# Modulation rows summed in the values stage, and a quarter of the retention gate made by block products

## The chip, the cores and the metric

The kernel runs on one core of a Trainium2 chip. The metric is the device time of one execution in microseconds (us). The engines of the core are called PE (TensorE, matrix products), DVE (VectorE), ACT (ScalarE), POOL (GpSimd) and SP (SyncE, which here does nothing but issue DMAs, one after the other). Each engine works through its own instructions in order.

## What is computed

One decoder block over a sequence of 1024 tokens, width 1024, float32. A conditioning vector gives six modulation vectors; the input is normalized and modulated to h; then two branches, retention and dilated attention, are gated, merged and followed by an MLP. What matters here, cut from the reference:

```python
mod = jax.nn.silu(c) @ w_ada[l] + b_ada[l]
sh1, sc1, g1, sh2, sc2, g2 = jnp.split(mod, 6, axis=-1)
h = modulate(rms_norm(x, norm1_g[l]), sh1, sc1)
...
proj = h @ w_in                                  # rq, rk, rv, rg, then attention and gates
rq = rotary(heads(rq, RET_HEADS), pos)
rk = rotary(heads(rk, RET_HEADS), pos) * (RET_DK ** -0.5)
ro = retention(rq, rk, heads(rv, RET_HEADS))     # 4 heads, chunks of 128 tokens, a state handed on
...
ro = (ro * gn_g.astype(jnp.float32) + gn_b.astype(jnp.float32)).astype(h.dtype)
ret_out = (jax.nn.silu(rg) * ro) @ w_ret_out
```

`mod` has 6 x 1024 values, held as 48 columns of 128: "row" i below is the block of w_ada (128 x 1024, 512 KB) that gives column i. Rows 0 to 15 (sh1, sc1) are needed for h; rows 16 to 47 (g1, sh2, sc2, g2) only after the attention. The retention gate rg has 2048 columns: 4 heads of four blocks of 128.

## The kernel before

**Products.** Every operand is split into a high and a low half (ACT rounds the high one, DVE subtracts for the low one), and a product is three matmuls (`mm3`, L203): low by high, high by low, high by high. A plain projection block of 128 columns (`proj_mm`, L472) takes 8 k x 2 token halves x 3 = 48 matmuls of 128 x 128 by 512. Pairs of blocks can be made in the other way, by seven products instead of eight of half-size blocks (`Blocks`, L226): 7 x 4 x 3 = 84 matmuls for two blocks of columns, with sums of weight blocks and of results done by DVE.

**Order of stages.** The order is written out by hand. After the first values come the *queries and keys* (`queries_keys`, L1216): 20 pairs from the list `PAIRS` (L1138), retention (r), attention (a, k) and gates (g), each by seven products. A result is finished in `a_out` (L1167); those that are not used at once are stored in DRAM. Then the *retention values* (`values`, L1339): ten items i, five products for each of two head pairs, in four slots p of 12 matmuls each. After `v_mm(i, p)` the loop runs `v_post` of the slot before (L1298) and the weight split of the next item: `v_w` on ACT (L1274) in the slots 0 and 1, `v_low` on DVE (L1280) in 1 and 2. The results of the products s3 and 22, in a high and a low half, go to a tile `vo` and from there to DRAM. For the first head pair these are items 2 and 3, and their tiles come from the pool `raw` (L1315); later ones come from other memory. At item 7 the first loads of the next stage are started.

Then the *chunks* (`chunk`, L692): 4 heads x 8 chunks of 128 tokens. In each, PE makes the chunk's key-value products (`kv`), a part of a gate block `rg` (plain, 8 k over two chunks), the scores of the next chunk (`s_kt`, L630), the output `o` from state and scores, the transpose of the last chunk's output (`on_T`, L669) and another part of the gate. DVE updates the state, splits it, and normalizes `o`; in the first four chunks of the next head, `u_final` (L680) multiplies by the gate tile `srg` (L689). With each chunk go the loads of its step (L1393): a gate weight in every other chunk and about one modulation row per chunk, which `mod_prep` (L461) multiplies by the conditioning vector and sums, one pass of DVE over 1024 elements.

**Buffers.** The pool for loaded weights and rows, tag `raw`, has three buffers of 512 KB (`wraw`, L150). A tile takes a buffer that an earlier tile has given up, in the order of the program, and what writes it waits until the earlier tile's last use is over, a store in DRAM included. The chunks' tiles lie on the memory that the values' tiles (`x`, 26 buffers) had (`open_ret`, L508; `chunk_tiles`, L620).

Of the kernel before, what the change touches and what calls it, by code (L numbers as in the profile page):

```python
# [21 lines left out]
H = 4  # L22
# [118 lines left out]
def block_kernel(ctx, tc, io, stop=None, dbg=None):  # L141
# [24 lines left out]
    def ps_mm(name):  # L166
        return PS["p"].tile([P, 2, 512], F32, tag="mm", bufs=2, name=name)
# [436 lines left out]
    def flat(ps):  # L604
        return ps.rearrange("p a b -> p (a b)")
# [14 lines left out]
    def chunk_tiles():  # L620

        p = R["p"]
        R["j"] = p.tile([P, 2, 4, C], F32R, tag="j", bufs=2, name="j2")
        R["sm"] = p.tile([P, C], F32, tag="sm", bufs=1, name="sm00")
        for n in ("smh", "sml"):
            R[n] = p.tile([P, C], F32R, tag=n, bufs=2, name=n + "00")
        for n in ("kh", "kl"):
            R[n] = p.tile([P, 2, P], F32R, tag=n, bufs=1, name=n + "00")

    def s_kt(i):  # L630

# [48 lines left out]
    def u_final(h, es=range(4), queue=nc.sync):  # L680
        for e in es:
# [7 lines left out]
            nc.vector.tensor_mul(t, t, hd["srg", h, e])  # L689
            queue.dma_start(y_d[h][:, 2 * (i % 2):2 * (i % 2) + 2, e // 2], t.rearrange("p (t x) -> p t x", t=2))  # L690

    def chunk(h, c, ahead, w=None):  # L692
        p = R["p"]
        g = NC * h + c
        if g + 3 < NG:
            fetch(g + 3)
        if c % 2 == 0:
            hd["rgw"] = w
            hd["rgp"] = ps_mm(f"rg{h}{c}")

        ks = {0: (5, 6, 6), 1: (6, 7, 8)}.get(g) or [4 * (c % 2) + i for i in (0, 2, 4)]
        if g == 0:
            proj_mm(hd["rgp"], hd["rgw"], range(2))
            s_kt(0)
            proj_mm(hd["rgp"], hd["rgw"], range(2, 5))
        vh, vl = hd["v", g][:, 0], hd["v", g][:, 1]
        st, sh, sl = R["state"], R["sh"], R["sl"]
        kvs = []
        if c < NC - 1:
            kh, kl = hd["k", g]  # L710
            for i in range(2):
                kv = ps_s(f"kv{h}{c}{i}")
                mm3([kv], (kh[:, i, :], kl[:, i, :]), [(vh, vl)], True, True)
                kvs.append(kv)
        if g == 0:
            s_kt(1)
        proj_mm(hd["rgp"], hd["rgw"], range(*ks[:2]))
# [12 lines left out]
        if 0 < g < NG - 1:  # L730
            s_kt(g + 1)
        po = ps_s(f"o{h}{c}")
        if c > 0:
            t = hd["j", g]
            for i in range(2):
                mm3([po], (t[:, 0, i, :], t[:, 1, i, :]), [(sh[:, i, :], sl[:, i, :])], i == 0, False)
        mm3([po], hd["s", g], [(vh, vl)], c == 0, True)
        for i in range(2) if g == 0 else ():
            nc.scalar.copy(st[:, i, :], kvs[i])
        if g > 0 and c < NC - 1:  # L740
            for i in range(2):
# [28 lines left out]
    va_d = [dram.tile([S, 512], F32, name=f"vad{g}") for g in range(3)]  # L770
    aq_d = {(p, g, a): dram.tile([P, S], F32, name=f"aqd{p}{g}{a}") for p in range(2) for g in range(3) for a in range(2)}
    ak_d = {(p, a): dram.tile([P, S], F32, name=f"akd{p}{a}") for p in range(2) for a in range(2)}
    h12_d = [dram.tile([P, 2, 512], F32, name=f"h12d{m}") for m in range(4)]
    xn, wa = [], []

# [359 lines left out]
    a_pairs = [("a", g, p) for p in range(2) for g in range(3)]  # L1135
    g_pairs = [("g", i) for i in range(len(GATES) // 2)]
    k_pairs = [("k", 2, p) for p in range(2)]
    PAIRS = [{"r": r_pairs, "a": a_pairs, "g": g_pairs, "k": k_pairs}[i].pop(0) for i in "rargrarkrargrarkgaga"]  # L1138
    NA = len(PAIRS)
    OA = {}  # L1140

    def a_load(q, part):
        pair = PAIRS[q]
        src = io[{"g": "w_gate2", "a": "w_aq", "k": "w_ak2"}.get(pair[0]) or f"w_r{pair[1]}"]
# [22 lines left out]
    def a_out(q, n, x, y=None):  # L1167

        pair = PAIRS[q]
        if q not in OA:  # L1170
            OA[q] = [x4(f"qa{q}{i}") for i in range(2)]
        i, t = int(n[0]) - 1, int(n[1]) - 1
        o, view = OA[q][i][:, 512 * t:512 * t + 512], lambda z: z
        if pair[0] in "ak" and pair[1] == 1:
            o = OA[q][i].rearrange("p (r n i) -> p r n i", r=4, n=2)[:, :, t, :]
            view = lambda z: z.rearrange("p (i r) -> p r i", r=4)
        elif pair[0] in "ak" and pair[1] == 2:
            o = OA[q][i].rearrange("p (r i) -> p r i", r=8)[:, :, 64 * t:64 * t + 64]
            view = lambda z: z.rearrange("p (i r) -> p r i", r=8)
        f = AF.Sigmoid if pair[0] == "g" else AF.Copy  # L1180
        if y is None:
            nc.scalar.activation(o, view(x), f)
        else:
            (nc.vector.tensor_add if n == "12" else nc.vector.tensor_sub)(o, view(x), view(y))
            if pair[0] == "g":
                nc.scalar.activation(o, o, f)
        if n in ("12", "21"):
            if pair[0] == "g":
                dst = gate_d[GATES[2 * pair[1] + i]]
            elif pair[0] == "a":  # L1190
                dst = aq_d[pair[2], pair[1], i]
            elif pair[0] == "k":
                dst = ak_d[pair[2], i]
            else:
                return
            nc.sync.dma_start(dst, OA[q][i])
# [136 lines left out]
    def v_base_load(hp):  # L1333

        for j in range(2):
            V["m", hp, j] = t = x4(f"vm{hp}{j}")
            nc.sync.dma_start(t.rearrange("p (a b) -> p a b", a=2), m11_d[hp][:, 2 * j:2 * j + 2])

    def values(ahead):  # L1339
        last = len(VSEQ) - 1  # L1340
        for i, (hp, n) in enumerate(VSEQ):
            if i + 2 <= last:
                v_load(i + 2)
            for p in range(4):
# [32 lines left out]
        for g in (1, 2):  # L1377
# [7 lines left out]
    steps.add(more_values, manual=True)  # L1385
    steps.add(queries_keys, manual=True)

    later_mods = [G1 + k for k in range(NK)] + [SH2 + k for k in range(NK)] + \
                 [SC2 + k for k in range(NK)] + [G2 + k for k in range(NK)]
# [1432 lines left out]
def pack(x, c, w_ada, b_ada, norm1_g, w_in, rel_bias, ret_gn_g, ret_gn_b,  # L2822
# [17 lines left out]
        "w_rg": _cols(w[:, 4096:6144]),  # L2840
# [33 lines left out]
```

## Time and profile before

| | before |
|---|---|
| time, median of 3 runs | 2176.75 us (2176.67 to 2182.43) |
| time of the profiled execution | 2179.79 us |
| its span in the profile | 2178.0 us |
| PE busy | 2151.7 us, 99% |
| DVE busy | 1512.8 us, 69% |
| ACT busy | 947.4 us, 43% |
| DMA, all queues | 420.98 MB, mean 193 GB/s |

The profile shows one execution: the instructions of each engine with their start, their length, and what ended the wait before them. A row such as `L464 DVE ... raw<-raw,cb` names the line of the kernel, the engine, and the tile written and those read. "To landing" is the time from the issue of a DMA until its data are there. PE's busy time counts overlapping matmuls once, so it says when PE had work, not how fast the work went; the granted clock (PEclk, 1.0 is full) says that.

### The profile page before, as it was taken

To read this page: it belongs to the slowest core of one execution; us is meant where nothing else is said; L and a number is where in the kernel's file an instruction comes from. 1 tells how busy PE (TensorE), PEld (TensorE's weight loads), DVE (VectorE), ACT (ScalarE), POOL (GpSimd) and SP (SyncE) were. 2 spreads that over 40 slices of the span, in tenths; PEclk is the share of its full clock that TensorE was granted. 3 is DMA by queue.
4 is the path that set the end of the run, shared out by engine and by line. 5 is a ranking of instruction groups with operands and counts; after the bars stand their busy time and mean duration, and the time that the engine had idled before them with its cause. 6 is when DMAs were issued, how large, how long until landed. Compare 5 with 4: busy or idle time off the path is not lost. (4 is left out here: it accounts for less than half of the span.)

```text
span 2178.0 us, 27354 instructions
## 1 busy us (share of the span) xinstructions
PE 2151.7 (99%) x10060; PEld 1789.6 (82%) x10060; DVE 1512.8 (69%) x2361; ACT 947.4 (43%) x1741; POOL 167.2 (8%) x199
## 2 busy tenths in 40 slices
PE   8999999999999999999999999999999999999998
PEld 6888888888887888888888888888778888888887
DVE  5885777776346787785657644777876665877855
ACT  5553322323343354455657625434454445533413
POOL 0001111100002121211110000001000000000003
PEclk9999999999999999999999999999999999999999
DMA  9759998833568455546777275653244435645322
GB/s 383 282 212 311 270 334 255 235 110 116 184 240 295 160 203 182 173 168 196 205 192 209 98 260 196 222 188 136 66 179 153 153 136 195 248 138 174 109 87 78
DMA packets 161522, 420.98 MB, mean 193 GB/s; under 512 B 27877, under 2 KB 55788, under 8 KB 158316
## 3 DMA queue, kind: packets, MB, share of 16 engines
q1 hardware_dynamic: 149112, 370.70, 47.7%
q0 software_dynamic: 9584, 48.24, 9.8%
q8 instruction: 79, 1.29, 0.2%
q10 hardware_dynamic: 2692, 0.30, 0.1%
q14 instruction: 55, 0.45, 0.1%
HBM read 322.03 MB, written 158.23 MB: 221 GB/s over the span
## 5 line engine op out<-in xcount | busy, mean ns | idle before, releaser
L207 PE MATMUL qap<-hh,qaw 128*128 128x512 f32 x240 | 93.4, 389 | 0.0
L209 PE MATMUL qap<-hl,qaw 128*128 128x512 f32 x240 | 93.4, 389 | 0.0
L211 PE MATMUL qap<-hh,qaw 128*128 128x512 f32 x240 | 93.4, 389 | 0.0
L617 POOL TENSOR_TENSOR j<-qk,j 128x512 fp32r<-128x512 f32 x32 | 43.2, 1351 | 457.5 <-ACT j L616 457.5
L2193 POOL TENSOR_TENSOR accnf<-accnf,sqnf 128x256 f32<-128x256 f32 (+1 forms) x18 | 16.6, 921 | 609.6 <-ACT sqnf L2189 609.6
L2297 ACT ACTIVATE a<-a 128x512 f32<-128x512 f32 x48 | 30.3, 631 | 73.3 <-DVE a L2296 73.3
L2505 ACT CAST w2h<-w2s 128x512 fp32r<-128x512 f32 x36 | 22.4, 621 | 78.7 <-DVE w2s L2543 71.8
L264 DVE TENSOR_TENSOR fw<-w1r,fw 128x512 fp32r<-128x512 f32 x48 | 32.9, 688 | 33.5 <-ACT fw L254 33.5
L209 PEld LDWEIGHTS qap<-hl,qaw 128*128 128x128 f32 x240 | 45.0, 188 | 9.4
L211 PEld LDWEIGHTS qap<-hh,qaw 128*128 128x128 f32 x240 | 45.0, 188 | 9.3
L207 PEld LDWEIGHTS qap<-hh,qaw 128*128 128x128 f32 x240 | 45.0, 188 | 9.3
L652 ACT COPY sm<-sT 128x128 f32<-128x128 f32 x32 | 8.5, 265 | 98.9 <-PE sT L640 91.4
L2028 DVE TENSOR_TENSOR rwl<-rwl,rwh 128x1024 fp32r<-128x1024 f32 x25 | 30.2, 1221 | 29.0 <-ACT rwh L2058 29.0
L207 PE MATMUL fp<-h2h,fw 128*128 128x512 f32 x128 | 50.0, 391 | 0.0
L211 PE MATMUL fp<-h2h,fw 128*128 128x512 f32 x128 | 49.8, 389 | 0.0
L209 PE MATMUL fp<-h2l,fw 128*128 128x512 f32 x128 | 49.8, 389 | 0.0
L207 PE MATMUL roa<-rh,rwl 128*128 128x512 f32 x128 | 49.8, 389 | 0.0
L209 PE MATMUL roa<-rl,rwh 128*128 128x512 f32 x128 | 49.8, 389 | 0.0
L211 PE MATMUL roa<-rh,rwh 128*128 128x512 f32 x128 | 49.8, 389 | 0.0
L1561 ACT ACTIVATE P<-P,ng 128x128 f32<-128x128 f32 (+1 forms) x96 | 41.9, 438 | 17.5 <-DVE ng L1553 17.5
L264 DVE TENSOR_TENSOR qaw<-wa,qaw 128x512 fp32r<-128x512 f32 x60 | 40.0, 686 | 8.8 <-ACT qaw L254 8.8
L292 DVE TENSOR_TENSOR qat<-qat,qap 128x512 f32<-128x512 f32 x20 | 13.7, 687 | 46.4 <-PE qap L211 46.4
(3094 smaller groups left out, 7241.4 us busy)
## 6 DMA issues: line engine op xcount, KB each, us to landing
v<-vd SPq DMA_DIRECT2D x32, 512.0 KB, 4.3
raw<-in_w_ada_dram SPq DMA_DIRECT2D x32, 512.0 KB, 5.0
w1r<-in_w_ff_dram SPq DMA_DIRECT2D x32, 512.0 KB, 4.6
yt<-y POOLq DMA_DIRECT2D x24, 512.0 KB, 7.4
xsd<-as SPq DMA_DIRECT2D x24, 512.0 KB, 2.9
w2r<-in_w_ff2s_dram SPq DMA_DIRECT2D x24, 512.0 KB, 6.7
em<-in_w_ada_dram SPq DMA_DIRECT2D x16, 512.0 KB, 10.2
wrvs<-in_w_rv_dram POOLq DMA_DIRECT2D x16, 512.0 KB, 9.6
```

Of the source, the lines that this page charges most:

```text
L207: nc.tensor.matmul(o, wl, xh, start=first, stop=False, skip_group_check=skip)
L209: nc.tensor.matmul(o, wh, xl, start=False, stop=False, skip_group_check=skip)
L211: nc.tensor.matmul(o, wh, xh, start=False, stop=last, skip_group_check=skip)
L264: nc.vector.tensor_sub(t[:, 512:], src, fv(t[:, :512]))
L292: nc.vector.tensor_sub(u, u, b)
L617: nc.gpsimd.tensor_sub(t[:, 1], src, fv(t[:, 0]))
L652: nc.scalar.copy(sm, ps[:, :C])
L1561: nc.scalar.activation(v, v, AF.Exp, bias=ng[:, blk:blk + 1], accum_out=st[:, g, blk, 2 + a:3 + a])
L2028: nc.vector.tensor_sub(lo, fv(lo), fv(hi))
L2193: (nc.vector if f == 7 else nc.gpsimd).tensor_add(G["acc", key], G["acc", key], sq)
L2297: nc.scalar.activation(o, o, AF.Relu)
L2505: nc.scalar.copy(hi, src)
```

## The change

Three things change together.

1. *The gate.* Of the four gate blocks of a head, the last is taken out of the chunks. The four blocks so taken (one per head) form two pairs, kind "s", at the end of `PAIRS`; they are made by seven products with the queries and keys, go through Silu and are stored in `srg_d`. In chunk 6 of each head the finished block is loaded (512 KB). The chunks do 24 k per head instead of 32, three per chunk (other numbers in head 0), and a gate weight is loaded at chunks 0, 2 and 5.
2. *The modulation rows.* 29 of the 32 rows 16 to 47 are loaded and summed in the values stage: six in each of the items 0 and 1, five in each of the items 4, 5 and 6, two in item 7. `values_mod(i)` starts the load of row i and does the pass of the row before the last one. The additions of the bias become one for all. Three rows stay in the chunks.
3. *The order of the chunks' first tiles.* `j` (two buffers of 4 KB per partition) is taken after the small tiles `sm`, `smh`, `sml`, `kh`, `kl` instead of before.

```diff
     def chunk_tiles():
...
-        R["j"] = p.tile([P, 2, 4, C], F32R, tag="j", bufs=2, name="j2")
         R["sm"] = p.tile([P, C], F32, tag="sm", bufs=1, name="sm00")
...
+        R["j"] = p.tile([P, 2, 4, C], F32R, tag="j", bufs=2, name="j2")
...
+    RG = ((6, 2, 2, 3, 3, 3, 3, 2),) + ((3,) * NC,) * (H - 1)
+
+    def rg_mm(n):
+        for _ in range(n):
+            if hd.get("rgk", NK) == NK:
+                hd["rgk"], hd["rgw"], hd["rgp"] = 0, hd["rgws"].pop(0), ps_mm("rg")
+            proj_mm(hd["rgp"], hd["rgw"], [hd["rgk"]])
+            hd["rgk"] += 1
+            if hd["rgk"] == NK:
+                hd["rgs"] = hd["rgp"]
+
+    def rg_out(h, c):
+        if "rgs" in hd:
+            e = {1: 0, 2: 0, 4: 1, 5: 1, 7: 2}[c]
+            hd["srg", h, e] = etile(f"srg{h}{e}")
+            nc.scalar.activation(hd["srg", h, e], flat(hd.pop("rgs")), AF.Silu)
+        if c == 6:
+            hd["srg", h, 3] = etile(f"srg{h}3")
+            nc.sync.dma_start(hd["srg", h, 3], srg_d[h])
...
-        proj_mm(hd["rgp"], hd["rgw"], range(*ks[:2]))
+        rg_mm(1 if g == 0 else RG[h][c] - 1)
...
-        proj_mm(hd["rgp"], hd["rgw"], range(*ks[1:]))
+        rg_mm(0 if g == 0 else 1)
...
-        if c % 2 == 1:
-            hd["srg", h, c // 2] = etile(f"srg{h}{c // 2}")
-            nc.scalar.activation(hd["srg", h, c // 2], flat(hd["rgp"]), AF.Silu)
+        rg_out(h, c)
...
-    PAIRS = [{"r": r_pairs, "a": a_pairs, "g": g_pairs, "k": k_pairs}[i].pop(0) for i in "rargrarkrargrarkgaga"]
+    s_pairs = [("s", i) for i in range(H // 2)]
+    PAIRS = [{"r": r_pairs, "a": a_pairs, "g": g_pairs, "k": k_pairs, "s": s_pairs}[i].pop(0)
+             for i in "rargrarkrargrarkgagass"]
...
+    MODS = [(i, p) for i in (0, 1, 4, 5, 6, 7) for p in range(4) if i < 7 or p < 2
+            for _ in range(2 if i < 2 and p % 2 or p == 3 else 1)]
+    NV = len(MODS)
+
+    def values_mod(i):
+        if i < NV:
+            t = V["mod", i] = wraw.tile([P, 1024], F32, tag="raw", name=f"vmod{i}")
+            nc.sync.dma_start(t, io["w_ada"][G1 + i])
+        if i > 1:
+            t, m = V.pop(("mod", i - 2)), G1 + i - 2
+            nc.vector.scalar_tensor_tensor(t, t, 1.0, cb, op0=ALU.mult, op1=ALU.mult, accum_out=mods[:, m:m + 1])
+        if i == NV + 1:
+            m = mods[:, G1:G1 + NV]
+            nc.vector.tensor_add(m, m, vec[:, VC_BADA + G1:VC_BADA + G1 + NV])
...
     def values(ahead):
...
                 if p == 2 and i < last:
                     v_low(i + 1, 1)
+                for j, at_ in enumerate(MODS):
+                    if at_ == (i, p):
+                        values_mod(j)
+                if (i, p) == MODS[-1]:
+                    values_mod(NV)
+                    values_mod(NV + 1)
...
-                      ([wsplit(io["w_rg"][4 * h + c // 2])] if c % 2 == 0 else []) +
-                      [mod_load(later_mods[8 * h + i]) for i in ({0: (0, 1), 1: ()}.get(8 * h + c, (c,)))],
+                      ([wsplit(io["w_rg"][3 * h + (0, 2, 5).index(c)])] if c in (0, 2, 5) else []) +
+                      ([later_mod()] if h > 0 and c == 4 else []),
```

More of the change, by code (lines that the diff above doesn't have):

```diff
@@ L696, in chunk @@
             fetch(g + 3)
[L697 to L701, printed above, removed]
+        if w is not None:
+            hd.setdefault("rgws", []).append(w)
         if g == 0:
-            proj_mm(hd["rgp"], hd["rgw"], range(2))
+            rg_mm(2)
             s_kt(0)
-            proj_mm(hd["rgp"], hd["rgw"], range(2, 5))
+            rg_mm(3)
         vh, vl = hd["v", g][:, 0], hd["v", g][:, 1]
@@ L772, in block_kernel @@
     ak_d = {(p, a): dram.tile([P, S], F32, name=f"akd{p}{a}") for p in range(2) for a in range(2)}
+    srg_d = [dram.tile([P, S], F32, name=f"srgd{h}") for h in range(H)]
     h12_d = [dram.tile([P, 2, 512], F32, name=f"h12d{m}") for m in range(4)]
@@ L1143, in a_load @@
         pair = PAIRS[q]
-        src = io[{"g": "w_gate2", "a": "w_aq", "k": "w_ak2"}.get(pair[0]) or f"w_r{pair[1]}"]
+        src = io[{"g": "w_gate2", "a": "w_aq", "k": "w_ak2", "s": "w_rg2"}.get(pair[0]) or f"w_r{pair[1]}"]
         i = 2 * pair[1] + pair[2] if pair[0] == "a" else pair[-1]
@@ L1179, in a_out @@
             view = lambda z: z.rearrange("p (i r) -> p r i", r=8)
-        f = AF.Sigmoid if pair[0] == "g" else AF.Copy
+        f = {"g": AF.Sigmoid, "s": AF.Silu}.get(pair[0], AF.Copy)
         if y is None:
@@ L1184, in a_out @@
             (nc.vector.tensor_add if n == "12" else nc.vector.tensor_sub)(o, view(x), view(y))
-            if pair[0] == "g":
+            if pair[0] in "gs":
                 nc.scalar.activation(o, o, f)
@@ L1193, in a_out @@
                 dst = ak_d[pair[2], i]
+            elif pair[0] == "s":
+                dst = srg_d[2 * pair[1] + i]
             else:
@@ L1386, in block_kernel, with later_mod @@
     steps.add(queries_keys, manual=True)
-    later_mods = [G1 + k for k in range(NK)] + [SH2 + k for k in range(NK)] + \
-                 [SC2 + k for k in range(NK)] + [G2 + k for k in range(NK)]
+    late_mods = iter(range(G1 + NV, 48))
+    def later_mod():
+        return mod_load(next(late_mods))
     for h in range(H):
@@ L2839, in pack @@
         "w_rv": _vblocks(w[:, 2048:4096]),
-        "w_rg": _cols(w[:, 4096:6144]),
+        "w_rg": _cols(w[:, 4096:6144].reshape(1024, 4, 4, P)[:, :, :3].reshape(1024, 1536)),
+        "w_rg2": _pairs(w[:, 4096:6144].reshape(1024, 4, 4, P)[:, :, 3].reshape(1024, 512)),
         "w_aq": _pairs(att[:, :, 0].reshape(1024, 1536)),
```

## The prediction

> **What bounds the kernel now.** First the page, for how full each engine is:
>
> ```profile
> span 2178.0 us, 27354 instructions
> PE 2151.7 (99%) x10060; PEld 1789.6 (82%) x10060; DVE 1512.8 (69%) x2361; ACT 947.4 (43%) x1741; POOL 167.2 (8%) x199
> ```
>
> TensorE (PE) is busy for all but 26 us, so a gain must be a matmul less or a part of those 26 us, and a loss is any wait that PE doesn't have today. Next the busy time by stretch around the stages that change: queries and keys until 561, retention values until 671, chunks until 985.
>
> ```profile
> core 0: us, PE busy (x) PEld busy (x) DVE busy (x) ACT busy (x) POOL busy (x), PEclk, DMA share, GB/s
> 190.00:555.00 365.00, 365.00 (x1612) 302.20 (x1612) 262.29 (x408) 104.17 (x183) 34.92 (x49) 1.00 0.73 226
> 583.00:605.00 22.00, 22.00 (x99) 18.22 (x98) 11.86 (x15) 8.70 (x12) 0.00 (x0) 1.00 0.63 220
> 671.00:701.00 30.00, 26.32 (x117) 20.96 (x118) 15.47 (x36) 11.36 (x25) 3.75 (x4) 0.94 0.73 258
> 701.00:985.00 284.00, 284.00 (x1386) 236.29 (x1385) 227.88 (x477) 132.26 (x336) 53.53 (x57) 1.00 0.53 176
> ```
>
> PE is full in each but the first chunks (671 to 701), where 3.7 us are missing and the granted clock is 0.94. VectorE (DVE) is at 54% in the middle of the values stage, so 29 more passes seem to have room there; it is at 80% in the chunks, from where they come. Last the timeline of PE, for what one matmul costs. A duration is 0.39, but they overlap; the starts count.
>
> ```profile
> 402.90 0.39 PE L207 MATMUL qap<-hh,qaw 128*128 128x512 f32 x1
> 403.13 0.39 PE L209 MATMUL qap<-hl,qaw 128*128 128x512 f32 x1
> ...
> 805.33 0.61 PE L207 MATMUL rg<-hh,raw_6146l 128*128 128x512 f32 x2
> ...
> 808.05 0.28 PE L638 MATMUL sT<-j 128*128 128x256 f32 x1
> ```
>
> In the queries and keys it is 0.227 us from start to start, and in the chunks twelve gate matmuls take 808.05 - 805.33 = 2.72, the same 0.227. A slot of the values stage (item i, part p: twelve matmuls) is 2.72 us, an item of four slots 10.9.
>
> **The matmuls: -5.4 us.** A gate block is 8 x 6 = 48 matmuls; four blocks fewer in the chunks are 192. Two pairs by seven products add 2 x 7 x 12 = 168. So 24 go, 24 x 0.227 = 5.4 us. The pairs' sums, splits and results lie under PE work where VectorE has 262 of 365 us busy: I cost them at nothing (uncovered, 14 splits by the row below, 0.69 each, would be 10 us). The pairs' two stores and the four loads of finished gate rows in chunk 6 are spread over stages whose DMA share is 0.5 to 0.7: nothing.
>
> ```profile
> L264 DVE TENSOR_TENSOR qaw<-wa,qaw 128x512 fp32r<-128x512 f32 x60 | 40.0, 686 | 8.8 <-ACT qaw L254 8.8
> ```
>
> **The chunks: 0.** They lose 192 x 0.227 = 43.6 us of PE work, so VectorE must be tested as the bound.
>
> ```profile
> L464 DVE SCALAR_TENSOR_TENSOR raw<-raw,cb x32: 1216/1218/1221, 659.5 to 972.1; 128x1024 f32<-128x1024 f32 x32
> L464 DVE DVE_READ_ACCUMULATOR raw<-raw,cb x32: 80/82/85, 660.6 to 973.2; 128x1 f32 x32
> ```
>
> ```profile
> 800.32 0.16 DVE L466 TENSOR_TENSOR mods<-mods,vec 128x1 f32<-128x1 f32 x1
> ```
>
> A row costs VectorE 1.22 + 0.08 + 0.16 = 1.46 there. With about 28 rows and four weight splits (1.22) less, VectorE falls from 228 to 228 - 41 - 5 = 182 us and PE from 284 to 240, so its share goes from 80% to 76%: still behind PE. I take 0; the bad end is 6 us, half a microsecond in each of the twelve chunks that also have a final multiply (L689).
>
> **The start of the chunks: -2 us.** Who is waited for at 671 to 701:
>
> ```profile
> PE kv L207 <- DVE kl L666: 3.1, 2, 2.5
> ```
>
> ```profile
> ACT sm L652 <- DMA vd<-vr: 7.4, 1, 7.4
> ```
>
> ```profile
> 681.00:686.00 5.00, 4.63 (x17) 3.92 (x18) 0.97 (x4) 0.68 (x3) 0.00 (x0) 0.66 1.03 352
> ```
>
> `sm` takes the memory of a tile whose store (`vd<-vr`) has not landed; behind it ACT's split of `kT` is late, `kl` too, PE idles 2.5 us, and in the five microseconds after that the granted clock is 0.66, another 0.34 x 5 = 1.7 us. The change puts the small tiles on other bytes and starts two 512 KB loads fewer ahead of them (three weights and one, for two weights and four rows). That could take away all 4.2 us, none, or, if the new place is held longer, cost up to 3. I take half the gain, 2.
>
> **The values stage: where I expect the time to go.** All loads here go through the pool `raw`, which has three buffers (L150). Today only the results of items 2 and 3 of the first head pair use it (L1315): eight tiles, one per slot, three in turn. The change runs the modulation rows through the same three buffers, with each pass two rows behind its load, and has no rows in items 2 and 3. At the end of item 1 rows 10 and 11 are loaded and not yet summed; their passes come in item 4. So **two of three buffers are held through items 2 and 3, and eight results share one.** Each must have landed in DRAM before ACT may write the next. What such a result costs today:
>
> ```profile
> 586.02 0.69 DVE L1322 TENSOR_TENSOR vr<-vr,va 128x512 f32<-128x512 f32 x1 [8.07 <-PE va L211]
> ...
> 586.74 0.62 ACT L1323 CAST vo<-vr 128x512 fp32r<-128x512 f32 x1 [1.89 <-DVE vr L1322]
> ...
> 588.12 6.54 SPq L1326 DMA_DIRECT2D vd<-vo  x3
> ...
> 606.96 0.60 ACT L1317 ACTIVATE vo<-va 128x512 fp32r<-128x512 f32 x1 [3.19 <-DMA vd<-vo]
> ...
> 610.17 1.22 DVE L1283 TENSOR_TENSOR vwl<-vwl,vwh 128x1024 fp32r<-128x1024 f32 x1
> ...
> 615.74 0.39 PE L207 MATMUL vc<-vwh,xat 128*128 128x512 f32 x1
> ```
>
> ```profile
> DMA to landing us min/median/max: 2.6/7.2/12.0
> ```
>
> ```profile
> aqd<-qa SPq DMA_DIRECT2D x12, 512.0 KB, 3.1
> ...
> y<-on SPq DMA_DIRECT2D x12, 512.0 KB, 3.2
> ```
>
> From ACT's copy to the issue of the store is 588.12 - 586.74 = 1.4 us; the stores of this line land after 2.6 to 12 us. A turn of a single buffer is thus 1.4 + landing, 4.0 at the least, against 2.72 for a slot. Even with three buffers the last two of the eight wait for a store today (606.96: 3.19 us). Stores of the same size in quieter stages land after 3.1 and 3.2; with only one result under way at a time I take 3.2 for six of the seven turns, and the median 7.2 for the one that meets the weight and base loads around item 3's start: 7 x 1.4 + 6 x 3.2 + 7.2 = 36.2 us from the first result's copy to the eighth's.
>
> The first result is late too. Ten passes stand ahead of it on VectorE, and item 0 starts when other loads are being issued:
>
> ```profile
> 564.42 0.93 SPq L1272 DMA_DIRECT2D vwl<-wrvs  x2
> ```
>
> ```profile
> raw<-in_w_ada_dram SPq DMA_DIRECT2D x32, 512.0 KB, 5.0
> ...
> vwl<-wrvs SPq DMA_DIRECT2D x12, 512.0 KB, 6.5
> ```
>
> The first row is issued at about 565.4 and lands after some 6.5, at 572. A buffer is then loaded (5.0) and read (1.3) before its next load, three in turn: one pass per 2.1 us. The tenth ends at 572 + 9 x 2.1 + 1.3 = 592.2, and the result's first operation, which was at 586.0, is 6.2 late (bounds 0, if loads keep pace, and 13).
>
> So the eighth copy is at 592.9 + 36.2 = 629.1 instead of 606.96. Behind it on ACT is the weight split of item 5, behind it on VectorE the split's low half (610.17 to 611.4 today: 4.4 after that copy) and now row 10's pass (1.3): PE can start item 5 at 629.1 + 5.7 = 634.8, not at 615.74. That is **+19.1 us**. With every store at 2.6 and no lateness: 586.74 + 28 + 5.7 = 620.4, +4.7. With 7.2 each: 592.9 + 60.2 + 5.7 = 658.8, +43.1. From item 4 on there are five rows an item, 5 x 1.3 us of VectorE beside results and weight splits, and SP's in-order queue has row loads ahead of weight loads; at the end two passes wait for loads just issued. I add 3 (0 to 9).
>
> **Sum:** -5.4 + 0 - 2 + 19.1 + 3 = +14.7 us. On the profiled execution (2179.8, of which 2178.0 are span) that is 2194.5; it lies 3.0 above the median of the runs, so on the median I say 2176.75 + 14.7 = **2191.4**.
>
> **Rivals.** (1) *The single buffer doesn't bind*, because the pool hands out memory otherwise than I read it, and the rows go where VectorE has room: -5.4 - 4.2 = 2167.2. For it: VectorE's 54%. Against it: three buffers, two of them unread, by the order of the code. This one ends faster. (2) *It binds but is mostly covered*: stores at 2.6, no lateness, -5.4 - 2 + 4.7 = 2174.1. For it: the first `vo` store today lands after 2.6; against it, the loads in the way. (3) *Stores as slow as today's median*: -5.4 - 2 + 43.1 + 3 = 2215.5. Against it: that median was measured with several in flight. (4) *The clock falls in the gaps*: as at 681, where 2.5 us idle cost 1.7 more. If three gaps of that length stand ahead of items 3, 4 and 5, 3 x 1.7 = 5 more: 2196.4. The Trainium skill (TensorE: Matmul & The Clock Gate, Part 1) has the array at half clock after one idle window of about 3.4 us, and for about as long after work resumes. This trace shows less idle time as enough (2.5 us). By the rule as written only gaps over 3.4 us would count. (5) *VectorE bounds the chunks*: up to 6 more, 2197.4; 182 of 240 us speaks against it.
>
> **Chances.** My forecast 0.54, (4) 0.08, (5) 0.02, (3) 0.13, (2) 0.10, (1) 0.13. About 0.3%, 6.5 us, is what a measurement tells from no change: below 2170.2 is faster, 0.13; (2) lies within, 0.10; the rest, 0.77, is slower. The forecast's own range is 2183 to 2206. For 8 in 10 I leave out (1) and the upper half of (3): 2173 to 2214.
>
> **What would show it.** Right: ACT's wait for `vd<-vo` (6.1 us in two waits today) grows to some 15 to 25 us in seven; PE has idle time in the values stage, ahead of items 4 and 5, and DVE waits for `raw` loads in items 0 and 1; the stage is 120 to 135 us long instead of 110; PE has 24 matmuls fewer; the chunks as a whole take about 44 us less, without a new wait. Wrong: the results of items 2 and 3 follow each other at 2.7 us, or PE waits for `onm`, `sml` or `statel` in the chunks. If the queries-and-keys stage grows by more than 38 us (168 x 0.227), my free cover there was none.

## The result, and the profile after

The changed kernel takes 2214.49 us (median of 4 runs, 2213.65 to 2215.37), beside 2176.71 for the kernel before on the same chip: 1.017 times as long, with a 95% interval of 1.0158 to 1.0183. That is 37.8 us slower; the prediction said 14.7 slower, with a range that ended at 2214.

The page of the changed kernel, its first lines:

```profile
span 2213.3 us, 27355 instructions
PE 2154.4 (97%) x10036; PEld 1787.2 (81%) x10036; DVE 1524.5 (69%) x2361; ACT 953.2 (43%) x1757; POOL 167.9 (8%) x199
```

PE has its 24 matmuls fewer (10036 for 10060) and is idle for 59 us of the span instead of 26. The busy time by stretch shows where: the queries and keys, the first 22 us of the values stage, its end, and its last 10 us together with the chunks.

```profile
core 0: us, PE busy (x) PEld busy (x) DVE busy (x) ACT busy (x) POOL busy (x), PEclk, DMA share, GB/s
190.00:593.50 403.50, 403.50 (x1782) 334.21 (x1781) 284.55 (x440) 117.69 (x205) 34.92 (x49) 1.00 0.70 215
599.50:621.50 22.00, 18.45 (x82) 14.97 (x81) 9.82 (x13) 9.82 (x15) 0.00 (x0) 1.00 0.84 282
709.50:739.50 30.00, 20.41 (x83) 16.18 (x82) 20.87 (x30) 9.59 (x14) 6.33 (x7) 0.89 0.78 270
739.50:1022.50 283.00, 277.36 (x1357) 228.91 (x1356) 207.89 (x433) 136.23 (x355) 59.08 (x66) 1.00 0.50 167
```

The queries and keys are still full. The values stage, full before, now has holes at its start (second row) and at its end (third row, two thirds). The chunks, from 749.6 on, lack a little too. The length of each stage, from the start of its first matmul to the start of the next stage's:

| stage, us | before | after | difference |
|---|---|---|---|
| up to the queries and keys | 180.5 | 180.7 | +0.1 |
| queries and keys | 380.8 | 418.9 | +38.1 |
| values, with the step to the chunks | 109.7 | 150.0 | +40.3 |
| chunks | 315.8 | 273.2 | -42.6 |
| the rest, to the last matmul | 1184.4 | 1184.0 | -0.4 |

The sum is +35.5, beside 35.3 between the two spans (2213.3 - 2178.0), which also hold what comes behind the last matmul. The two profiled executions, 2179.79 and 2215.37 us, are 35.6 apart; the first is 3.1 above its median and the second 0.9 above its own, which makes the 37.8 of the medians.

The waits of the values stage that the prediction named, VectorE and ACT of the changed kernel (total, number, longest):

```profile
DVE vmod L1372 <- DMA vmod<-in_w_ada_dram: 19.9, 13, 4.2
...
ACT vo L1339 <- DMA vd<-vo: 15.6, 4, 5.5
...
ACT vo L1345 <- DMA vd<-vo: 13.5, 3, 6.2
```

ACT waits seven times for a result's store, 29.1 us. In the kernel before it was two times:

```profile
ACT vo L1317 <- DMA vd<-vo: 6.1, 2, 3.2
```

ACT's timeline in the changed kernel shows the chain, first copy and eighth:

```profile
633.55 0.62 ACT L1345 CAST vo<-vr 128x512 fp32r<-128x512 f32 x1 [6.64 <-DVE vr L1344]
...
641.35 0.62 ACT L1345 CAST vo<-vr 128x512 fp32r<-128x512 f32 x1 [6.21 <-DMA vd<-vo]
...
669.77 0.60 ACT L1339 ACTIVATE vo<-va 128x512 fp32r<-128x512 f32 x1 [3.81 <-DMA vd<-vo]
```

The first copy is 633.55 - 599.57 = 34.0 us into the stage, before 586.74 - 561.34 = 25.4: 8.6 late. From there to the eighth are 669.77 - 633.55 = 36.2 us. The timeline of PE, the longer waits and the start of item 5:

```profile
615.75 0.50 PE L209 MATMUL va<-vwlTrue,xat 128*128 128x512 f32 x1 [3.55 <-DVE vwlTrue L1307]
...
643.88 0.51 PE L209 MATMUL va<-vwl,hh 128*128 128x512 f32 x1 [3.46 <-DVE vwl L1307]
...
663.83 0.80 PE L209 MATMUL vc<-vwl,hh 128*128 128x512 f32 x1 [5.41 <-DVE vwl L1305]
...
675.43 0.39 PE L207 MATMUL vc<-vwh,xat 128*128 128x512 f32 x1
...
679.66 0.51 PE L209 MATMUL vc<-vwl,xat 128*128 128x512 f32 x1 [2.48 <-DVE vwl L1305]
...
726.95 0.79 PE L209 MATMUL va<-vwl,hh 128*128 128x512 f32 x1 [8.29 <-DVE vwl L1307]
```

Every one of them is a wait for the low half of a weight, which VectorE makes late. An item has two such halves: the first is needed at its second matmul, the other at its eighth. For the first wait shown, VectorE stood 4.24 us for a row's load, made the pass at 613.32 and the low half only at 614.47. Item 5 starts 75.86 us into the stage instead of 54.40: +21.5. Behind that another 18.8 are lost, 8.29 of them in the last wait. What VectorE does ahead of it:

```profile
719.85 1.23 DVE L1372 SCALAR_TENSOR_TENSOR vmod<-vmod,cb 128x1024 f32<-128x1024 f32 x1 [1.75 <-DMA vmod<-in_w_ada_dram]
...
722.33 1.23 DVE L1372 SCALAR_TENSOR_TENSOR vmod<-vmod,cb 128x1024 f32<-128x1024 f32 x1 [1.25 <-DMA vmod<-in_w_ada_dram]
...
725.68 1.22 DVE L1307 SCALAR_TENSOR_TENSOR vwl<-vwl,vwh 128x1024 fp32r<-128x1024 f32 x1
```

These are the last two rows, summed in the same slot in which the last load was started, and only then, behind a result, the second low half for item 8. The clock falls behind the longer gaps, by the busy time by stretch:

```profile
644.60:648.00 3.40, 3.40 (x10) 2.62 (x9) 1.29 (x2) 0.62 (x1) 0.00 (x0) 0.50 0.21 78
...
661.70:668.50 6.80, 4.67 (x11) 3.71 (x12) 2.51 (x3) 0.81 (x2) 0.00 (x0) 0.50 0.34 135
...
723.10:729.90 6.80, 2.95 (x7) 2.37 (x8) 4.97 (x9) 1.58 (x3) 0.00 (x0) 0.50 0.53 155
```

PE works 3.40 + 4.67 + 2.95 = 11.0 us at half the clock, which costs half of that, 5.5; 4.0 of it lies ahead of item 5. PE's waits for low halves in the stage are 31.4 us in all (16.2 up to item 5), so waits and clock together are 36.9 of the 40.3.

### The profile page after: what moved, and what is told of

It is laid out like the page before. It is cut to its first block, busy times and chain, and to the rows that moved or that the text cites. A ratio compares the mean times of both kernels' runs of the same rounds, so it can differ in the third digit from the quotient of the medians.

```text
span 2213.3 us, 27355 instructions
## 1 busy us (share of the span) xinstructions
PE 2154.4 (97%) x10036; PEld 1787.2 (81%) x10036; DVE 1524.5 (69%) x2361; ACT 953.2 (43%) x1757; POOL 167.9 (8%) x199
## 5 line engine op out<-in xcount | busy, mean ns | idle before, releaser
L209 PE MATMUL qap<-hl,qaw 128*128 128x512 f32 x264 | 102.8, 389 | 0.0
L211 PE MATMUL qap<-hh,qaw 128*128 128x512 f32 x264 | 102.8, 389 | 0.0
L207 PE MATMUL qap<-hh,qaw 128*128 128x512 f32 x264 | 102.8, 389 | 0.0
L209 PEld LDWEIGHTS qap<-hl,qaw 128*128 128x128 f32 x264 | 49.6, 188 | 10.3
L207 PEld LDWEIGHTS qap<-hh,qaw 128*128 128x128 f32 x264 | 49.6, 188 | 10.3
L211 PEld LDWEIGHTS qap<-hh,qaw 128*128 128x128 f32 x264 | 49.6, 188 | 10.2
L1372 DVE SCALAR_TENSOR_TENSOR vmod<-vmod,cb 128x1024 f32<-128x1024 f32 x29 | 35.3, 1223 | 20.3 <-DMA vmod<-in_w_ada_dram 19.9
## 6 DMA issues: line engine op xcount, KB each, us to landing
wrvs<-in_w_rv_dram POOLq DMA_DIRECT2D x16, 512.0 KB, 10.3
```

Of the source, the lines that this page charges most:

```text
L207: nc.tensor.matmul(o, wl, xh, start=first, stop=False, skip_group_check=skip)
L209: nc.tensor.matmul(o, wh, xl, start=False, stop=False, skip_group_check=skip)
L211: nc.tensor.matmul(o, wh, xh, start=False, stop=last, skip_group_check=skip)
L1372: nc.vector.scalar_tensor_tensor(t, t, 1.0, cb, op0=ALU.mult, op1=ALU.mult, accum_out=mods[:, m:m + 1])
```

## The experiments

The theory after the result (A): the rows cost the time where they went, by waits and not by work: two of three `raw` buffers are held through items 2 and 3, passes stand in VectorE's queue waiting for their loads ahead of the weights' low halves, and the clock falls in the gaps. The rivals: the gate's products cost (B), the traffic of the moved loads costs (C), VectorE's extra work costs (D). The runs below were each timed beside the kernel before on the same chip (2176.0 to 2177.5 us in all of them).

### The parts by themselves

**gate_only.** The rows stay in the chunks' steps, the gate and the order of tiles are as after.

```diff
-                for j, at_ in enumerate(MODS):
-                    if at_ == (i, p):
-                        values_mod(j)
...
-                      ([later_mod()] if h > 0 and c == 4 else []),
+                      [later_mod() for _ in range({0: 2, 1: 0}.get(8 * h + c, 1))],
```

> The gate and the order of the first tiles as in the change; the modulation rows stay in the chunks, one per chunk, as before. Theory A (the rows in the values stage cost the time: one shared buffer, passes that wait for their loads ahead of other VectorE work, and the half clock behind each gap): the values stage is back at 110 us from 150; the 24 matmuls less show. VectorE has 9.3 us of work in the twelve chunks with a row and a final multiply, where PE has 8.7, so some of the gain goes there: 2172 to 2182 us. Theory B (the gate by seven products is the cost): 2200 us or more.

Measured 2191.0 us, ratio 1.0065 (1.005 to 1.008): slower, which A did not expect. The values stage is back at 109.7 us, so the 40 us are the rows'. But the chunks take 288.9 us. PE's waits in them, and VectorE in one of them:

```profile
PE o L207 <- DVE state L744: 9.0, 14, 0.8
PE kv L207 <- DVE kl L666: 5.6, 8, 1.1
```

```profile
865.42 1.22 DVE L689 TENSOR_TENSOR on<-on,srg 128x1024 f32<-128x1024 f32 x1
866.56 1.28 DVE L744 SCALAR_TENSOR_TENSOR state<-state,kv 128x512 f32<-128x512 f32 x2
867.75 1.22 DVE L198 TENSOR_TENSOR raw_6926l<-raw,raw_6926h 128x1024 fp32r<-128x1024 f32 x1
868.89 1.22 DVE L464 SCALAR_TENSOR_TENSOR raw<-raw,cb 128x1024 f32<-128x1024 f32 x1
```

With a quarter of the gate's products gone, the final multiply of the last head (L689) stands in VectorE's queue ahead of the state that PE needs next, and the row's pass ahead of the scores and `kl`. So the move of the rows was worth 288.9 - 273.2 = 15.7 us in the chunks, and it cost 40.3 in the values stage.

**loads_only** leaves out the 29 passes (the columns get a constant), **passes_only** leaves out the 29 loads (the passes read data that is there).

```diff
-            t, m = V.pop(("mod", i - 2)), G1 + i - 2
-            nc.vector.scalar_tensor_tensor(t, t, 1.0, cb, op0=ALU.mult, op1=ALU.mult, accum_out=mods[:, m:m + 1])
+            V.pop(("mod", i - 2))
...
```

```diff
-            t = V["mod", i] = wraw.tile([P, 1024], F32, tag="raw", name=f"vmod{i}")
-            nc.sync.dma_start(t, io["w_ada"][G1 + i])
+            V["mod", i] = cs
...
```

> The change without the 29 passes: the rows are loaded into the same buffers at the same places and not read (their sums are left out, a constant stands for them). A buffer is then free when its load has landed. Theory A: no pass waits and no buffer is held through items 2 and 3, so the values stage is 110 to 116 us and the time 2169 to 2178. Theory C (traffic): the stage stays above 130 us, 2195 or more. Theory D (VectorE's work): as A.

> The change without the 29 loads: the passes stand at the same places but read a tile that is already in SBUF (the sums are then of other data). Theory A: no pass waits, no buffer is held; the values stage is 110 to 115 us, since VectorE is at most 70% busy in any item but item 4 (14 of 11 us); 2168 to 2176. Theory C (traffic): as A. Theory D (VectorE's work): the stage stays above 130 us, 2195 or more.

Measured 2182.26 (1.0024, 1.0013 to 1.0034) and 2179.78 us (1.0015, 1.0005 to 1.0024). The values stage takes 114.6 and 113.4 us. So the traffic alone (C) costs 4.9 us, the work alone (D) 3.7; together they are far from 40. What neither run has is a pass that *waits for* a load, or a buffer that such a pass holds: the rest lies there. Both times lie some 4 us above A's range. The gate part, with the rows out of the chunks, doesn't gain what I had it gain: queries and keys and chunks together give +38.1 - 42.6 = -4.5, and that only against a profile of before that had a stall in its chunks, as the next run shows.

**before_again**, the kernel before unchanged, a second profile.

> The kernel before, unchanged, for a second profile of it. Is the wait of 2.5 us at the start of its chunks, with the lower clock behind it, there in every execution? If the store that is late there is late by chance, this profile has less of it and a span of about 2175; if not, about 2178 again.

2179.5 us (one execution), span 2177.7. The chunks take 313.0 us instead of 315.8, and PE's waits in them for `kl` and the state are

```profile
PE kv L207 <- DVE kl L666: 1.4, 2, 0.7
...
PE o L207 <- DVE state L725: 0.2, 1, 0.2
```

The wait of 2.5 us with the lower clock behind it isn't there: not every execution has it. (The span is as long as in the first profile all the same; other stages took 2.5 us more.) Against this profile the chunks gain 313.0 - 273.2 = 39.8, and the gate part, with the rows out of the chunks, is worth 1.7 us.

### What the values stage waits for

**flush_two.** One edit: the two rows that lie unread through items 2 and 3 are summed at the end of item 1, so the eight results have three buffers.

```diff
-        if i > 1:
-            t, m = V.pop(("mod", i - 2)), G1 + i - 2
-            nc.vector.scalar_tensor_tensor(...)
+        done = (i - 2, 10, 11) if i == 11 else (i - 2,)
+        for j in done:
+            if ("mod", j) in V:
+                t, m = V.pop(("mod", j)), G1 + j
+                nc.vector.scalar_tensor_tensor(...)
```

> The change, but rows 10 and 11 are summed at the end of item 1 instead of in item 4, so that items 2 and 3 have all three buffers. Theory A: the seven waits of ACT for vd<-vo (29.1 us) shrink to about the 6 us of before; the eight results take about 20 us from first copy to last instead of 36.2; the first result is 5 us later, since its VectorE waits for two loads more; item 5 starts some 11 us earlier: about 2203 us. Theory C (the DMA traffic of the moved rows fills the stage): the waits move elsewhere and the time stays at 2212 to 2216. Theory D (VectorE has too much work in the stage): the same, 2212 to 2216.

Measured 2204.78 us, 1.0129 (1.0112 to 1.0146), as A said: 9.7 less. Item 5 starts 64.1 us into the stage instead of 75.9. The stage takes 135.0 us in the profiled execution, which was 3.5 us below the median, and ACT's waits for the results' stores are

```profile
ACT vo L1339 <- DMA vd<-vo: 7.8, 2, 4.6
```

**results_own.** The same buffers relieved from the other side: the results get two buffers of their own (the memory of the cosines and sines), the rows keep `raw` and all their slots.

```diff
-            t = wraw.tile([P, 2, DV], F32R, tag="raw", name=f"vo{i}{p}")
+            t = cs[:, p % 2].bitcast(F32R).rearrange("p (a b) -> p a b", a=2)
```

> The changed kernel with one edit: the eight results of items 2 and 3 go to two buffers of their own (the memory of the cosines and sines); the rows keep the three buffers of the pool raw and all their slots. A1, the one buffer left to the results costs most: ACT's waits for vd<-vo fall from 29 to under 10 us, the values stage from 150 to 133-137 us (as in flush_two), 2198-2206. A2, passes that wait for rows ahead of low halves cost most and the results' buffer lay beside that: the stage stays at 145-150 us, 2209-2214.

Measured 2203.65 us, 1.0124 (1.011 to 1.0138): A1's time. Item 5 starts 67.6 us into the stage. The stage takes 140.6 us, 4 more than A1 gave, in an execution 2.3 us above the median; ACT's waits for stores are 8.9 + 4.2 us in five, where A1 gave under 10:

```profile
ACT cossin L1339 <- DMA vd<-cossin: 8.9, 4, 4.3
ACT cossin L1345 <- DMA vd<-cossin: 4.2, 1, 4.2
```

The two runs agree in time: the one buffer is worth about 10 us, not the 19 that I gave to the stage up to item 5. Without it item 5 still starts 9.7 and 13.2 us later than before the change, since PE then waits for low halves that stand behind passes (3.41 us at 615.83 in flush_two, 4.10 at 615.99 in results_own).

**own_buffers.** The rows get the two buffers instead, in the same slots, with the pass of row i - 2 ahead of the load of row i; the results have `raw` to themselves.

```diff
-            t = V["mod", i] = wraw.tile([P, 1024], F32, tag="raw", name=f"vmod{i}")
-            nc.sync.dma_start(t, io["w_ada"][G1 + i])
+            nc.sync.dma_start(cs[:, i % 2], io["w_ada"][G1 + i])
...
```

> All 29 rows in the same slots of the values stage as in the changed kernel, but loaded into two buffers of their own (the memory of the cosines and sines, which nobody reads in this stage); the pool raw is left to the results, as before the change. A, the shared buffers: the eight results of items 2 and 3 no longer wait for one another, the waits of ACT for vd<-vo fall from 29 us to under 10 us and the values stage from 150 to 125-133 us, which gives 2188-2198. What is left above 110 us is then the passes that wait for their loads in VectorE's queue. C, the traffic of the rows, or D, VectorE's extra work: rows, bytes and passes are the same, so the time stays within 4 us of the changed kernel's 2214.

Measured 2213.45 us, 1.017 (1.0156 to 1.0184): no gain, a miss for A as I had put it. Up to item 5 it did what A says: item 5 starts 66.9 us into the stage, and PE has no wait in items 3 and 4. Before that and behind it the waits grew; from item 5 on the stage took 81.3 us instead of 74.2. The run changed two things, since the rows now have two buffers in turn and not three. SP's queue shows what that does in the first items:

```profile
604.59 17.51 SPq L1371 DMA_DIRECT2D cossin<-in_w_ada_dram  x6
622.16 0.90 SPq L1294 DMA_DIRECT2D vwl<-wrv  x2
```

Each load waits in SP's in-order queue for the pass that frees its buffer, and the weights' loads behind six of them are issued at 622. So what the results gained, the rows lost by pacing VectorE and SP.

**last_two_later.** One edit: the last two passes are issued in slot 3 of item 7 instead of slot 1, behind both low halves of item 8.

```diff
-                if (i, p) == MODS[-1]:
+                if (i, p) == (7, 3):
                     values_mod(NV)
                     values_mod(NV + 1)
```

> The changed kernel with the last two passes and the addition of the bias issued in slot 3 of item 7 instead of slot 1, that is behind both low halves of item 8's weights; nothing else differs. A, passes waiting ahead of low halves: the wait of 8.3 us ahead of item 8's first product with those halves goes, and most of the half clock of 6.8 us behind it (3.4 us worth), so the values stage takes 137-142 us instead of 150 and the time is 2202-2207. Rival, the wait there is for item 8's weights or the traffic and the pass only stands beside it: no change beyond 3 us, 2211-2215.

Measured 2208.88 us, 1.0148 (1.0131 to 1.0165); the stage takes 142.3 us, at the edge of what A gave, and the time is 5.6 less, 2 short of its range. The long wait has become

```profile
720.05 0.50 PE L209 MATMUL va<-vwl,hh 128*128 128x512 f32 x1 [2.60 <-DVE vwl L1307]
```

**flush_no_item7** goes on from flush_two: 27 rows, none in item 7, the last two summed at the end of item 6, and two rows more in chunks.

```diff
-    MODS = [(i, p) for i in (0, 1, 4, 5, 6, 7) for p in range(4) if i < 7 or p < 2
+    MODS = [(i, p) for i in (0, 1, 4, 5, 6) for p in range(4)
...
```

> The change with rows 10 and 11 summed at the end of item 1, and no rows in item 7: 27 rows in the values stage, the last two summed at the end of item 6; five in the chunks. Theory A: the wait of 7.4 us for the last two passes and the half clock behind it (6.8 us at half, 3.4) leave item 7; in item 6 results go to ACT alone and hide most of the same wait: 2193 to 2198 us, from 2204.8. Theory C or D: two rows less are 2 to 3 us, about 2202.

Measured 2201.08 us, 1.0112 (1.0097 to 1.0128), 3.7 less than flush_two where A expected 7 or more: the stage takes 133.1 us, PE waits eleven times for low halves, 16.1 us in all. The two passes still wait for loads just issued, one item earlier (1.21 and 0.91 us).

### Fewer rows, and the order of the tiles

**rows_in_cs.** 18 rows in the values stage, a load in every second slot, each pass three slots behind its load, in two buffers of their own; 14 rows in chunks without a final multiply. **rows_in_cs_jfirst** is the same with `j` taken first, as before the change. **rows_in_cs_late** is the first with the final multiply issued in the next chunk, behind the update of the state.

```diff
...
+                slot = 4 * i + p
+                if slot % 2 and 0 <= (slot - 3) // 2 < NV:
+                    row_pass((slot - 3) // 2)
+                if slot % 2 == 0 and slot // 2 < NV:
+                    row_load(slot // 2)
...
+                      ([later_mod()] if (h > 0 and c > 3 or h == 0 and c in (4, 6)) else []),
```

> The change, but only 18 rows are summed in the values stage, one in every second slot, in the 8 KB of cos and sin that are no longer needed (two buffers of their own, a row read three slots after its load is issued); the other 14 in chunks without a final multiply. Theory A: the traffic and the passes alone cost some 4 us each at 29 rows, the rest was the shared buffers and passes that stand waiting; so the values stage is 110 to 113 us, the chunks about 273 and the time 2170 to 2178. Theory C or D (traffic or VectorE's work): 18 of 29 rows still bring 0.6 of 40 us, about 2200.

> As the one with rows in the memory of cos and sin, with the order of the chunks' first tiles as before the change (j first). By my prediction the new order is worth 0 to 4.2 us at the start of the chunks; I expect 0 to 4 us more here, as a wait of PE for kl and a lower clock behind it. If the place of the tiles doesn't matter: no difference.

> As the one with rows in the memory of cos and sin, and the final multiply of a head's gate is issued after the state update of the next chunk instead of before it. If the waits of PE for the state (4.1 us in 11) come from the multiply that stands ahead of the update, they go: 4 us less than that kernel. If VectorE is simply full there, the wait moves to kl, onm or statel and the time stays.

Measured 2187.69 (1.0054, 1.0041 to 1.0066), 2187.84 (1.0055, 1.0043 to 1.0068) and 2214.12 us (1.017, 1.0156 to 1.0184), the first some 10 us above what A gave. Between the first two, the order of the tiles makes no difference. In the first, the values stage and the step to the chunks are 119.9 us, and the largest wait is at the end:

```profile
PE rg L207 <- DVE vr L1344: 6.2, 1, 6.2
```

```profile
707.61 1.23 DVE L1370 SCALAR_TENSOR_TENSOR cossin<-cossin,cb 128x1024 f32<-128x1024 f32 x1 [3.87 <-DMA cossin<-in_w_ada_dram]
```

This pass, in the last slot of item 8, waits 3.87 us for a row whose load was issued at 696.5, 11 us before, among the chunks' first loads (DMA share 1.03 to 1.07 from 700 to 708), and the last results stand behind it. The late multiply is a plain miss, 26 us slower. There, VectorE in a chunk and PE in all of them:

```profile
835.73 1.23 DVE L689 TENSOR_TENSOR on<-on,srg 128x1024 f32<-128x1024 f32 x1 [0.92 <-ACT on L687]
...
841.25 0.81 DVE L779 TENSOR_SCALAR onm<-o,ba,gr 128x512 f32<-128x512 f32 x1
```

```profile
PE kT L645 <- DVE onm L779: 20.3, 11, 2.5
```

It left its place ahead of the state and took one ahead of the normalization, for which PE waits longer.

**rows_14.** 14 rows, two per item in the slots 2 and 3, behind both low halves; each pass a whole item behind its load, none after item 7; the other 18 in chunks without a final multiply.

```diff
...
+                if p > 1:
+                    k = 2 * i + p - 2
+                    if 2 <= k < NV + 2:
+                        row_pass(k - 2)
+                    if k < NV:
+                        nc.sync.dma_start(cs[:, k % 2], io["w_ada"][G1 + k])
...
+                      ([later_mod()] if (h > 0 and c > 3 or h == 0 and c > 1) else []),
```

> Only 14 rows in the values stage, two per item in the slots 2 and 3, behind both low halves of the next weights, each pass a whole item (10.9 us) behind its load, in buffers of their own; none of the passes later than item 7. The other 18 rows are in chunks that have no final multiply. A, passes that stand in VectorE's queue ahead of low halves or of the last results while they wait for a load: no such wait is left, the values stage takes 111-115 us, the 6 us ahead of the first gate product and the half clock behind them are gone, the chunks take 273-276 us: 2172-2180. If the loads' traffic by itself cost (C), the stage would be at 117 us or more as with 18 rows, 2183-2188.

Measured 2182.42 us, 1.0024 (1.0015 to 1.0033). In the values stage A is right: 111.2 us, no low half later than 1.1 us and no half clock. The time misses A's range by 2.4 us; the chunks take 278.2 us, where A gave 273 to 276, and PE waits in them for the state and `kl`.

### The final multiply off VectorE

**gate_only_pool** and **rows_14_pool** are those two kernels with the final multiply of the chunks on GpSimd.

```diff
-            nc.vector.tensor_mul(t, t, hd["srg", h, e])
+            (nc.gpsimd if queue is nc.sync else nc.vector).tensor_mul(t, t, hd["srg", h, e])
```

> The gate part alone (all 32 rows in the chunks, as in gate_only), with the final multiply of a head's blocks on GpSimd in place of VectorE. If VectorE is late in the chunks because the multiply (1.22 us) stands ahead of the state's update, the waits for state and kl (14.6 us in gate_only) mostly go, the chunks take 271-276 us instead of 289, and the time is 2173-2179, beside 2177 before and 2191 for gate_only. If it is VectorE's total work that bounds the chunks, 15 us less of it in 289 gains at most 4 us: 2187 or more. If GpSimd's multiply makes VectorE slower or comes late itself, 2190 or more.

> rows_14 with the final multiply on GpSimd. The same reason: the waits for state and kl in the chunks (6.7 us) mostly go, the chunks take 271-274 us instead of 278, and the time is 2174-2178. If VectorE's total work bounds them, no change beyond 1 us (2181-2183).

Measured 2182.2 (1.0025, 1.0015 to 1.0035), which is 8.8 less than gate_only, and 2173.2 us (0.9983, 0.9974 to 0.9992), which is 9.2 less than rows_14: **faster than both kernels**, by 4.3 us (0.2%) than the one before. The first missed its range by 3.2 us, the second ended 0.8 below its own. All waits of PE of 0.3 us or more in rows_14_pool, from the values stage to the end of the chunks:

```profile
PE rg L207 <- DVE vr L1344: 0.8, 1, 0.8
PE kT L645 <- DVE onm L777: 0.7, 1, 0.7
PE kv L207 <- DVE kl L666: 0.6, 1, 0.6
PE vc L209 <- DVE vwl L1305: 0.5, 1, 0.5
PE kv L207 <- ACT state L758: 0.5, 1, 0.5
PE o L207 <- DVE state L744: 0.3, 2, 0.2
```

The chunks take 270.4 us and the values stage 110.6. With a row in nearly every chunk (gate_only_pool, 280.7 us) the state is in time, and what is left is the wait for `kl`:

```profile
PE kv L207 <- DVE kl L666: 8.4, 12, 1.1
```

So the multiply on VectorE made the state late, and the rows' passes make `kl` late (0.6 us with 18 of them, in chunks without a multiply, 8.4 with 32). VectorE's total work as the limit, the rival there, gave 2187 or more and 2181 or more, and falls. How much of the 8.4 comes from passes that GpSimd slows (last section) is not separated.

## Why the prediction was wrong

**The matmuls, -5.4: right.** The queries and keys grew by 38.1 us, 168 x 0.227, with PE full: the cover held in that stage.

**The chunks, 0: too good.** Of 43.6 us of products that went, 39.8 came off (by the second profile of before). In the changed kernel PE has a new wait there:

```profile
PE o L207 <- DVE state L744: 4.1, 11, 0.6
```

The state's wait before was 0.2. This is within the 6 us that I kept as the bad end, and nine of the eleven are at the place I named (the chunks with a final multiply). VectorE's share of 76% said nothing on it; what counts is what stands in its queue ahead of the one value that PE needs.

**The start of the chunks, -2: no term at all.** In the second profile of before the wait was absent. I costed a stall that one of two executions had. The order of the tiles, tried with 18 rows in the values stage, makes no difference; on the kernel before it was not tried.

**The values stage to item 5, +19.1: right in size, in part by luck.** Measured +21.5. The first result was 8.6 late (6.2 predicted), and the eight follow in 36.2 us, with two long turns (7.8 and 7.1) and five of 4.0 to 4.4 where I had one of 8.6 and six of 4.6. That the single buffer makes it so is shown by flush_two and results_own. That these other turns add up to the predicted 36.2 is luck. And the path was another: item 5 starts 5.7 after the eighth copy, as I said, yet PE does not wait there. It had stopped earlier, 5.9 us in items 1 and 2 for low halves behind passes and 10.3 in items 3 and 4 for low halves behind results; the longest, 5.41 at 663.83, is behind the sixth copy (661.32). Another 4.0 us are the clock, which the term did not hold. So it isn't the buffer's alone: without it the time falls by 10 to 11 us, not 19.

**The failed step: "I add 3 (0 to 9)", for what comes from item 4 on.** Measured behind item 5's start: 18.8, and so a stage of 150 us and not of 120 to 135. I named the parts, five passes an item, row loads ahead of weight loads and two passes that wait for loads just issued, and gave no working for the 3. They had to be priced at what stands behind them: a low half of a weight, for which PE stops. PE's waits for low halves behind item 5's start are 15.3 us in six, and the clock is another 1.5. The rows quoted above give 2.48 and 8.29 for two of the six; last_two_later takes the second down to 2.60 and the time by 5.6 us.

**The clock, rival (4), was no rival but a part of the terms:** three stretches at half clock, in items 3, 4 and 8, 5.5 us where I had 5 for items 3 to 5. They lie inside the +21.5 and the +18.8. The rule of the Trainium skill (TensorE: Matmul & The Clock Gate, Part 1), half clock after one idle window of about 3.4 us, agrees with the three gaps here that had it behind them, 3.46, 5.41 and 8.29 us. It does not fit the gap of 2.60 us in rows_in_cs, behind which PE ran at half clock from 658.4 to 661.9:

```profile
658.83 0.79 PE L209 MATMUL vc<-vwl,xat 128*128 128x512 f32 x1 [2.60 <-DVE vwl L1305]
```

```profile
658.40:661.90 3.50, 3.07 (x7) 2.48 (x8) 2.81 (x6) 0.62 (x1) 0.00 (x0) 0.51 0.95 341
```

A gap of the same 2.60 us in last_two_later (quoted above) had no half clock behind it (granted clock 1.00 from 717 to 724), and neither had the 3.55 us that end at 615.75 in the changed kernel (1.00 in the row from 599.5 to 621.5). So in these runs the length of a gap alone does not say whether the clock falls.

**The sum of the terms as measured,** by profile: -5.4 for the matmuls, +1.0 in the chunks (42.6 came off where 43.6 of products went), +21.5, +18.8 and -0.3 in the other stages: 35.6, beside 35.3 between the spans. What stays open: how the 40 us of the values stage divide between the buffer and the waiting passes, since each hides part of the other (taken alone, 10 to 11 and 5.6 us); why flush_no_item7 gained no more than 3.7; and what decides whether the clock falls behind a gap.

## What to carry to other kernels

Work that waits costs what stands behind it in its engine's queue: price a moved instruction by the next value in that queue for which the bound engine stops, not by the idle share of the engine that does it. If data is loaded for it, put the pass as far behind its load as the buffers allow and behind what is urgent, and never leave a loaded buffer of a shared pool unread through a stage that uses the pool. And before a stall is counted as a gain, see it in a second execution.

## What was not expected of the hardware

GpSimd takes about twice VectorE's time for the final multiply, and it slows VectorE beside it. By line, in rows_14_pool (minimum, median and maximum in ns):

```profile
L689 POOL TENSOR_TENSOR on<-on,srg x12: 2392/2404/2417, 791.4 to 950.1; 128x1024 f32<-128x1024 f32 x12
L689 DVE TENSOR_TENSOR on<-on,srg x4: 1224/1226/1227, 989.0 to 993.2; 128x1024 f32<-128x1024 f32 x4
```

```profile
L464 DVE SCALAR_TENSOR_TENSOR raw<-raw,cb x18: 1210/1220/2351, 728.2 to 970.4; 128x1024 f32<-128x1024 f32 x18
```

The passes that took 2.35 us, three of them, are those that began 1.1 us into a multiply on GpSimd; the others took 1.22. One such pair, from the timelines of GpSimd and VectorE:

```profile
808.29 2.40 POOL L689 TENSOR_TENSOR on<-on,srg 128x1024 f32<-128x1024 f32 x1 [1.09 <-ACT on L687]
```

```profile
809.42 2.35 DVE L464 SCALAR_TENSOR_TENSOR raw<-raw,cb 128x1024 f32<-128x1024 f32 x1
```

The Trainium skill (GPSIMD Engine Reference, Specifications) says that GpSimd shares its SBUF interfaces with VectorE, with contention where VectorE reads two inputs from there, as this pass does; this trace agrees, 2.35 us for 1.22.
